# Scores over 64 features: the product with the key's lo part on 128 rows instead of 64

## The chip, the cores and the metric
The kernel runs on one core of one Trainium2 chip. The metric is the device time of one execution in microseconds; before the change three runs gave a median of 3492.87 us (3492.13 to 3494.03).

## The reference
The program computes four layers on 512 tokens of 2048 features in float32 and a last RMS norm: a layer of gated linear attention and forgetting attention, a state-space layer, a layer of a gated linear recurrence and sliding-window attention ("even"), and a layer of latent attention (MLA) and differential attention ("odd"). Every layer is a norm, a large projection, the mixers, a gate and an output projection, with the old stream added.

The change touches three score products, all of them over 64 features:
- sliding window: 16 query heads, 2 key heads of 64 features; a query block of 128 sees its own and the preceding 128 keys. `s = einsum(q, k) * 64 ** -0.5`, mask, softmax with a sink.
- MLA: 8 heads; a score is a product over 128 features of the head plus one over 64 rotary features whose key all heads share, scaled by 192 ** -0.5, causal mask, softmax.
- differential attention: 8 heads with two components of 64 features each; two causal softmaxes per head, of which one is subtracted from the other with the weight lambda. A norm over each head's 128 outputs (the "subnorm") follows.

## The kernel before
**Numbers.** A float32 operand is split into two parts of a shorter float format (float32r): hi, the rounded value, and lo, what is left. A product is then hi x hi + hi x lo + lo x hi (`PARTS`, L270), three matmuls that add in one accumulator. In projections (`chunkF` L272, `chunkT` L289) the weights are read by DMA into `wraw`, split into `whl` by ScalarE (hi) and VectorE (lo), and multiplied with the split activations `hl`; a piece's matmuls use one stationary tile twice in a row. Their accumulators are the four `pj` buffers.

**Scores over 64 features.** Two heads (or two components) lie on the two halves of the 128 partitions. `stack_q` (L210) makes one tile for each of the two: the hi part of the query in its own 64 rows, the lo part in the other 64. `stack_k` (L219) makes for each a tile with the key's hi part in both halves, and one more tile that holds the two lo parts, each in its own half. One matmul on 128 rows then gives (hi + lo) x hi; a second one on 64 rows, over the half in which the query's hi part lies, gives hi x lo. `stacked` (L228) returns these two pairs of operands:

```python
    def stacked(self, i, q, k, lo):
        h = self.HALF[i]
        return [(q, k), (q[h], lo[h])]
```

The hi copies are ScalarE's (`self.act`), the lo parts GpSimd's (`eng=self.nc.gpsimd`, called POOL in the profile).

**Where they are used.** In `layer_even`, `ev_kv` (L1279) writes both the hi and the lo part of each key head to both halves (tiles `kd` of tag hb, `kl` of tags acc and acc2). `pair` (L1302) handles two heads: for every two query tiles and each head it adds the mask by a matmul with the identity, then the two products, in one `sc` accumulator of 512 columns; softmax on VectorE and ScalarE, transposes through `tr`, value products into `po`. In `layer_odd` the rotary key is projected twice side by side (L1434 on), so `kr` (hi, tag hb) and `krl` (lo, tag acc) hold it in both halves. `mla_group` (L1459) handles two heads: projections of keys, values and queries, then for each head and each of four query tiles the plain float32 product over 128 features, the two stacked products over 1 to 4 blocks of 128 keys, and the mask (`causal_scores` L532), softmax (`softmax_tile` L510), transposes, and the value products (`pv` L541). `diff_group` (L1484) handles two heads of the differential attention: two projections with `stack_q` and `stack_k` as evacuation (tags ha for the queries and the keys' hi parts, hc for the lo parts), the value projection, then for each head and query tile two score tiles (the two components), and after the four tiles the value products and the subnorm. The subnorm squares the output, splits the square (`parts` L350, tiles of tag hc), sums it over the partitions by a matmul with ones (`rsqrt_bcast` L356) and takes the reciprocal root.

**Buffers.** The tags have fixed numbers of buffers (L109): ha 8, hb 3, hc 4, wk 4 (work tiles: evacuations and the probabilities), acc, acc2 and fac one each; accumulators pj 4, sc 2, tr 1, po 1 (L111). acc2 holds `kv_bc` and fac `q_bc` while MLA's projections run. A tile of a tag waits until an older one of that tag is no longer read.

**Order.** The program is written head by head, but the order on each engine is made by a planner (L1589), which simulates the instructions by its own costs. It puts projections of the next group between the score tiles of the group before, so TensorE works on projections while a softmax runs. Each engine takes its list in order.

Of the kernel before, what the change touches and what calls it, by code (L numbers as in the profile page):

```python
# [11 lines left out]
F32 = mybir.dt.float32  # L12
F32R = mybir.dt.float32r
# [4 lines left out]
ALU = mybir.AluOpType  # L18
# [14 lines left out]
def shape_constants():  # L33
    """Arrays that depend on shapes alone: identity, masks, rotary tables."""
# [31 lines left out]
def layout(inputs):  # L66
    """The arrays as the kernel reads them: activations by features, vectors along features as
    columns of 128, the state-space layer's by pairs of groups. Nothing is computed."""
# [31 lines left out]
class Net:  # L100
# [57 lines left out]
    @contextmanager  # L158
    def after(self, instructions):
        """Keeps what is traced inside behind these instructions on their engine."""  # L160
        with ExitStack() as st:
            for i in instructions:
                st.enter_context(self.tc.issue_after(i.ins))
            yield

# [33 lines left out]
    def split(self, dst_hi, dst_lo, src, g=None):  # L199
        """dst_hi + dst_lo = src (* g), exactly to float32."""  # L200
        if g is None:
            self.act(dst_hi, src)
            self.tt(dst_lo, src, dst_hi.bitcast(F32), ALU.subtract)
        else:
            self.act(dst_hi, src, scale=g)
            self.stt(dst_lo, src, g, dst_hi.bitcast(F32), ALU.mult, ALU.subtract)
# [3 lines left out]
    def stack_q(self, x, tags):  # L210
        """x holds two operands of 64 rows. Each gets a tile: its hi part in its own rows, its lo
        part in the others."""
        out = [self.hd(tag, F32R) for tag in tags]
        for i, h in enumerate(self.HALF):
            self.act(out[i][h], x[h])
            self.tt(out[i][self.HALF[1 - i]], x[h], out[i][h].bitcast(F32), ALU.subtract, eng=self.nc.gpsimd)
        return out

    def stack_k(self, x, tags):  # L219
        """The partners of stack_q: for each operand its hi part twice, and the lo parts in place."""  # L220
        out = [self.hd(tag, F32R) for tag in tags]
        for i, h in enumerate(self.HALF):
            for h2 in self.HALF:
                self.act(out[i][h2], x[h])
            self.tt(out[2][h], x[h], out[i][h].bitcast(F32), ALU.subtract, eng=self.nc.gpsimd)
        return out

    def stacked(self, i, q, k, lo):  # L228
        """Operands of product i: (hi + lo) * hi, then hi * lo."""
        h = self.HALF[i]  # L230
        return [(q, k), (q[h], lo[h])]

    def split_all(self, raws, gname=None, perm=False):
        """Sixteen tiles [P, S] to hi and lo parts."""
# [13 lines left out]
    CW = 256  # L248

    def wpiece(self, src, k0, n, ncol):  # L250
        """Rows of n k-tiles, split: [P, 2 parts, k-tiles, columns]."""
# [8 lines left out]
    def wcols(self, w, *segs):  # L260
        """Source of weight columns: segs are (start, width) put side by side."""
# [10 lines left out]
    def chunkF(self, h, nk, src, ncol, evac):  # L272
        """Weights stationary; evac(f, ps) gets ps [128 features, tokens]."""
# [15 lines left out]
    def chunkT(self, h, nk, src, ncol, evac):  # L289
        """Activations stationary; evac(t, ps) gets ps [128 tokens, ncol]."""  # L290
# [21 lines left out]
    def bcast(self, tok, bc=None, tag="tr"):  # L312
        """[128 tokens, 4] to [128, 512], the same row in every partition."""
# [14 lines left out]
    def colsum(self, accs, perm=False, tag="tr"):  # L328
        """Sum of accs over partitions, as [128 tokens, 4] in PSUM."""
# [8 lines left out]
    def rsqrt(self, ss, dim, mul=None):  # L338
        """rsqrt(ss / dim (* mul) + EPS) for [128, 4]."""
# [10 lines left out]
    def parts(self, x):  # L350
        hi, lo = self.hd("hc", F32R), self.hd("hc", F32R)
# [4 lines left out]
    def rsqrt_bcast(self, dim, parts, tag, bc=None):  # L356
        """rsqrt of the column sums of parts / dim + EPS, the same row in every partition."""
# [25 lines left out]
    def silu2(self, ps, bc, out=None):  # L383
        """2 * silu(ps * bc)."""
# [16 lines left out]
    def gate(self, kt0, bc):  # L401
        """Evacuation of gates: alone where they come first, else times the mixer's output."""
# [10 lines left out]
    def put(self, kt, o, col=None, row=None):  # L413
        """A mixer's output o (* col * row) to its place, times the gate if that is there."""
# [28 lines left out]
    def w_out(self, h, w, perm=False, fac=None, fold=None, store=True, beside=None):  # L443
        """x + mix @ w, feature-major. fac: factor of the old x by tokens.
        fold: gain that the new x is kept multiplied with."""
# [40 lines left out]
    def final_out(self, raws, acc, gname, out):  # L486
        """out = x * rsqrt * g."""
# [11 lines left out]
    def transpose_into(self, pt, t, probs, n, eng):  # L499
        """The n blocks of probs [128 q, n * 128], transposed, to pt's columns of tile t."""  # L500
# [9 lines left out]
    def softmax_tile(self, n, scores, scale, bias=None, rowmul=None):  # L510
        """Softmax over the n * 128 keys of one tile of queries. scores(ps) makes the
        products and the mask. Returns exp parts, 1 / sum (times rowmul)."""
# [19 lines left out]
    def causal_scores(self, t, pairs):  # L532
        """pairs: (q, k) [K, 512] operands whose products are added."""
# [7 lines left out]
    def pv(self, pt, v):  # L541
        """o [128 dv, 512]: v(kt) [128 keys, 128 dv]."""
# [9 lines left out]
    def layer_ab(self, raws, beside=None):  # L552
# [40 lines left out]
        # The first values go with the narrow columns: g_lr to rows 0-15, f_f to rows 32-39.  # L593
# [13 lines left out]
        # Decays of GLA: 16 * log_a, cumulated within chunks of 64.  # L607
# [14 lines left out]
        # log forget gates of the second attention, on partitions 32-39.  # L622
# [16 lines left out]
        # Sums of whole chunks between a token and the middle of a level's block.  # L639
# [20 lines left out]
        def gla_scores(hh):  # L660
# [3 lines left out]
            # diagonal  # L664
# [9 lines left out]
            for li, s in enumerate(LEVELS + (128, 256)):  # L674
# [9 lines left out]
                else:  # L684
# [4 lines left out]
                    for half, op in ((0, ALU.subtract), (1, ALU.add)):  # L689
                        # an access pattern keeps at most three free dimensions  # L690
# [133 lines left out]
    def s5_params(self):  # L824
        """Discretised state matrices of the state-space layer. Pairs of groups share the
        partitions as (g2, p); four steps of time make one chunk of the recurrence."""
# [21 lines left out]
        # th modulo 2 pi  # L848
# [20 lines left out]
        # exp(a) - 1 and exp(a)  # L869
# [26 lines left out]
        # (Lambda - 1) / lambda  # L896
# [16 lines left out]
        # that times Lambda ** (3 - s), s = 0 .. 2  # L913
# [18 lines left out]
        # magnitude and phase of a chunk's decay  # L932
# [5 lines left out]
        # phases of n chunks: n = 16 a + b  # L938
# [8 lines left out]
        for tab, size in ((Tb, 16), (Ta, 8)):  # L947
# [5 lines left out]
            while m < size or nxt is None:  # L953
                # pw = phase ** m; entries m .. 2m - 1
# [19 lines left out]
        # by batches: tables of phases and the magnitudes  # L974
# [13 lines left out]
    def s5_batch_params(self, b):  # L988
        """Matrices of four pairs of groups, to DRAM: C * Lambda ** (t + 1) with rows (part, p)
        and columns (g, pair, t, c); Lambda ** (3 - s) * B, real and imaginary, with rows (g, s, c)  # L990
        and columns (pair, g, p); the products within a chunk with rows (g, s, c'), columns (pair, t, c)."""
# [16 lines left out]
        # Lambda ** (3 - s) * B  # L1008
# [15 lines left out]
        # C * Lambda ** (t + 1): real part and negated imaginary part  # L1024
# [11 lines left out]
        # products within a chunk of time: rows (pair, g, c'), columns (delay, c)  # L1036
# [19 lines left out]
    def s5_batch(self, b, U, dbc, z):  # L1056
        """Four pairs of groups: U [P n, 4 pairs, (g, s, c)] to z [P channels, (t, n)]."""
# [55 lines left out]
        # states before a chunk, by groups: rows (part, p)  # L1113
# [33 lines left out]
    def layer_c(self, raws, acc):  # L1147
# [9 lines left out]
        def advance(new=None):  # L1157
            """Second half of the batch under way, once the next one's first half is there."""
# [49 lines left out]
    def layer_even(self, raws, tok, bc):  # L1208
# [7 lines left out]
        # kap = -4 * softplus(-lambda)  # L1216
# [57 lines left out]
        # sliding-window attention: two heads in a pair share the partitions  # L1274
# [27 lines left out]
        def pair(j, q):  # L1302
            kv = j // 4
            po = self.ps("po")
            for tp in range(2):
                pT2 = self.t("pt", [P, 2, S])
                pTs = [pT2[:, 0], pT2[:, 1]]
                for hf in range(2):
                    sk = sink[:, 2 * j + hf:2 * j + hf + 1]
                    pb = self.ps("sc")  # L1310
                    for a in range(2):
                        t = 2 * tp + a
                        o = a * 256
                        if t:
                            self.mm(pb[:, o:o + 256], self.identb, mb[:, 0:256], stop=False)
                            for i, (l, r) in enumerate(self.stacked(hf, q[hf], kd[kv], kl[kv])):
                                self.mm(pb[:, o:o + 256], l[:, t * P:(t + 1) * P], r[:, (t - 1) * P:(t + 1) * P], start=False, stop=(i == 1))
                        else:
                            self.mm(pb[:, 0:P], self.identb, mb[:, 256:384])
                            self.mm(pb[:, P:256], self.identb, mb[:, 128:256], stop=False)  # L1320
                            for i, (l, r) in enumerate(self.stacked(hf, q[hf], kd[kv], kl[kv])):
# [59 lines left out]
    def layer_odd(self, raws, tok, bc):  # L1381
# [3 lines left out]
        # lambda of the differential attention, in every partition  # L1385
# [29 lines left out]
        # latent projections  # L1415
# [43 lines left out]
        def mla_group(gi):  # L1459
# [13 lines left out]
            for f in range(2):  # L1473
                pt = self.t("pt", [P, 1280])
                for t in range(4):
                    pr, r = self.softmax_tile(
                        t + 1, self.causal_scores(t, [(qn[f], kn[f])] + self.stacked(f, qr[f], kr, krl)), 192 ** -0.5)
# [6 lines left out]
        def diff_group(gi):  # L1484
            qk = [None] * 4

            def ev_qk(i):
                def e(f, ps):
                    x = self.wk()
                    self.tt(x, ps, bc, ALU.mult)  # L1490
                    qk[2 * i + f] = (self.stack_k(x, ("ha", "ha", "hc")) if f else self.stack_q(x, ("ha", "ha")))
# [6 lines left out]
            for f in range(2):  # L1498
                pt = self.t("pt", [P, 1280])
                for t in range(4):  # L1500
                    wd = (t + 1) * P
                    both = []
                    for comp in range(2):
                        q, k = qk[2 * f], qk[2 * f + 1]
                        both.append(self.softmax_tile(
                            t + 1, self.causal_scores(t, self.stacked(comp, q[comp], k[comp], k[2])), 64 ** -0.5))
# [8 lines left out]
                rb = self.rsqrt_bcast(P, self.parts(sq), "tr")  # L1515
# [77 lines left out]
```

## Time and profile before

| | |
|---|---|
| median of three runs | 3492.87 us |
| the profiled execution, its span | 3490.6 us, 2.3 us less than the median of the runs |
| TensorE matmuls | 3411.1 us busy, 98%, 18156 instructions |
| weight loads (PEld, beside the matmuls) | 2829.9 us, 81% |
| VectorE, ScalarE, GpSimd | 1896.3, 1326.0, 902.8 us (54%, 38%, 26%) |
| sliding window / MLA / differential | about 1880 to 2163, 2655 to 2860, 2860 to 3265 us of the span |

PE is TensorE's matmul, PEld its weight load, DVE is VectorE, ACT ScalarE, POOL GpSimd, SP SyncE. A line such as `sc<-hc,ha 64*128 64x256 f32` is an instruction that writes a tile of the tag sc, reads hc and ha, uses 64 rows and 128 columns of the array and streams 256 columns. The profile counts a matmul as busy until its modelled end, and matmuls overlap; the distance from one start to the next is what one costs in a stream.

### The profile page before, as it was taken

What the parts mean: (1) busy time and instruction counts of PE and PEld (TensorE: products, weight loads), DVE (VectorE), ACT (ScalarE), POOL (GpSimd) and SP (SyncE); (2) the same over time, 40 slices, a digit from 0 to 9 for tenths busy, and PEclk for the clock granted to TensorE, in tenths of its full rate; (3) what the DMA queues carried; (4) which work ended last, traced back from release to release, by engine and by line L of the source; (5) the groups of instructions that cost most, each with busy time, mean ns of one, the idle gap of its engine ahead of it and who ended that gap; (6) DMA issues with size and microseconds to landing.
All of it is one profiled execution on the core that took longest, in us unless ns stands there. A gap on an engine that the chain in (4) does not pass through costs nothing.

```text
span 3490.6 us, 49294 instructions
## 1 busy us (share of the span) xinstructions
PE 3411.1 (98%) x18156; PEld 2829.9 (81%) x18156; DVE 1896.3 (54%) x3165; ACT 1326.0 (38%) x2465; POOL 902.8 (26%) x1021
## 2 busy tenths in 40 slices
PE   8999999999989999999999999999999999999997
PEld 7898788877788888888887777888888787888886
DVE  5763543475579787634354555443544545546634
ACT  4443333232332323323343554232433444445422
POOL 2341800256767665100221100012110111111011
PEclk9999999999999999999999999999999999999998
DMA  4323333467734333333442222334332222232333
GB/s 138 81 64 86 100 96 88 117 175 223 229 111 118 117 111 108 118 118 119 144 130 82 61 70 84 95 118 144 105 92 75 67 70 73 78 80 73 106 117 110
DMA packets 402849, 374.48 MB, mean 107 GB/s; under 512 B 63896, under 2 KB 364312, under 8 KB 402608
## 3 DMA queue, kind: packets, MB, share of 16 engines
q1 hardware_dynamic: 399856, 368.38, 36.4%
q8 instruction: 142, 2.33, 0.3%
q10 hardware_dynamic: 2752, 2.96, 0.3%
q14 instruction: 99, 0.81, 0.1%
HBM read 333.36 MB, written 37.86 MB: 106 GB/s over the span
## 4 chain that ended last, share of the span: by engine, by line
PE 87%; DVE 6%; POOL 3%; issue 2%; DMA 1%; ACT 1%; SPq 0%; DVEq 0%; ACTq 0%; POOLq 0%
PE pj L152 77%; PE sc L152 6%; PE po L152 3%; PE tr L156 2%; DVE wk L1107 2%; DVE wk L140 1%; DVE whl L140 1%; POOL vs L140 1%; POOL wt L140 1%; PE tr L152 1%; DVE hl L143 0%; DMA s5d<-hc 0%; SPq L265 0%; POOL hc L140 0%; DMA wraw<-in_ab_w_in_dram 0%
## 5 line engine op out<-in xcount | busy, mean ns | idle before, releaser
L152 PE MATMUL pj<-hl,whl 128*128 128x512 f32 x10224 | 2457.2, 398 | 17.5 <-ACT whl L137 8.5
L152 PEld LDWEIGHTS pj<-hl,whl 128*128 128x128 f32 x10224 | 1912.2, 189 | 463.5 <-DVE whl L140 10.9
L140 DVE TENSOR_TENSOR whl<-wraw,whl 128x512 fp32r<-128x512 f32 (+2 forms) x1064 | 838.0, 790 | 1105.2 <-ACT whl L137 1098.9
L137 ACT ACTIVATE whl<-wraw 128x512 fp32r<-128x512 f32 (+2 forms) x1064 | 661.3, 623 | 1445.7 <-PE pj L152 1192.6
L152 PE MATMUL pj<-whl,hl 128*128 128x256 f32 (+1 forms) x3840 | 488.5, 287 | 16.7 <-DVE whl L140 10.6
L152 PEld LDWEIGHTS pj<-whl,hl 128*128 128x128 f32 x3840 | 475.6, 192 | 23.1 <-DVE whl L140 11.8
L140 POOL TENSOR_TENSOR acc<-acc,wt 128x512 f32<-128x512 f32 x88 | 125.6, 1433 | 861.6 <-ACT wt L137 859.9
L140 POOL TENSOR_TENSOR ha<-wk,ha 64x512 fp32r<-64x512 f32 x32 | 44.3, 1384 | 313.9 <-ACT ha L137 272.7
L137 ACT ACTIVATE wk<-sc,sm 128x256 f32<-128x256 f32 (+3 forms) x160 | 79.5, 501 | 62.2 <-DVE sm L148 59.4
L140 POOL TENSOR_TENSOR wt<-wt,acc 64x508 f32<-64x508 f32 x32 | 57.3, 1791 | 141.7 <-DVE wt L140 85.0
L140 POOL TENSOR_TENSOR wt<-ha,wk 128x256 f32<-128x256 f32 x72 | 63.2, 905 | 112.9 <-PE pj L152 59.6
L520 DVE TENSOR_REDUCE sm<-sc 128x1 f32<-128x128 f32 (+3 forms) x96 | 47.0, 490 | 77.9 <-PE sc L152 77.5
L140 POOL TENSOR_TENSOR hc<-wt,hc 128x512 fp32r<-128x512 f32 x12 | 15.6, 1298 | 276.6 <-issue 122.3
L152 PE MATMUL po<-pt,vs 128*128 128x128 f32 x560 | 80.3, 276 | 0.0
L156 PE MATMUL tr<-ident,wk 128*128 128x128 f32 x416 | 71.3, 279 | 7.9 <-DVE wk L143 6.8
L140 POOL TENSOR_TENSOR wt<-vs,vs 128x256 f32<-128x256 f32 x64 | 58.7, 941 | 70.6 <-DMA vs<-s5w 70.0
L1107 DVE TENSOR_TENSOR_SCAN wk<-pt,wk 128x128 f32<-128x128 f32 x128 | 75.9, 656 | 0.0
L152 PEld LDWEIGHTS po<-pt,vs 128*128 128x128 f32 x560 | 72.9, 191 | 2.3
L152 PE MATMUL sc<-ha,ha 128*128 128x128 f32 (+1 forms) x224 | 72.0, 391 | 2.3 <-DVE sm L524 2.2
L156 PEld LDWEIGHTS tr<-ident,wk 128*128 128x128 f32 x416 | 52.4, 143 | 23.0 <-issue 10.1
L137 ACT ACTIVATE pt<-tr 128x256 f32<-128x256 f32 (+2 forms) x80 | 40.6, 507 | 65.9 <-PE tr L156 65.7
L148 DVE TENSOR_SCALAR wk<-wk,sm 128x256 f32<-128x256 f32 (+3 forms) x160 | 60.1, 388 | 5.0
(300 smaller groups left out, 3006.4 us busy)
## 6 DMA issues: line engine op xcount, KB each, us to landing
wraw<-in_l_w_in_dram SPq DMA_DIRECT2D x272, 256.0 KB, 2.8
wraw<-in_ab_w_in_dram SPq DMA_DIRECT2D x216, 256.0 KB, 2.8
wraw<-in_c_w_in_dram SPq DMA_DIRECT2D x128, 256.0 KB, 2.8
wraw<-in_l_w_out_dram SPq DMA_DIRECT2D x128, 256.0 KB, 2.7
wraw<-in_ab_w_out_dram SPq DMA_DIRECT2D x64, 256.0 KB, 3.8
wraw<-in_glu_w_dram SPq DMA_DIRECT2D x64, 256.0 KB, 2.6
wraw<-in_c_w_out_dram SPq DMA_DIRECT2D x64, 256.0 KB, 2.6
wraw<-in_l_w_in_dram SPq DMA_DIRECT2D x128, 128.0 KB, 2.2
```

The source lines that it names most:

```text
L137: return self.nc.scalar.activation(out, in_, func, **kw)
L140: return (eng or self.nc.vector).tensor_tensor(out, a, b, op=op)
L148: return e.tensor_scalar(out, a, s1, None, op0=op0)
L152: return self.nc.tensor.matmul(out, l, r, start=start, stop=stop)
L156: return self.nc.tensor.transpose(out, in_, self.ident[:k, :k])
L520: self.nc.vector.tensor_reduce(mx, pb[:, 0:w], axis=AX.X, op=ALU.max)
L1107: nc.vector.tensor_tensor_scan(x[:, pq(q)], tab[:, 192 + q:193 + q].to_broadcast([P, P]), x[:, pq(q)], 0.0, op0=A.mult, op1=A.add)
```

## The change
`stacked` no longer cuts the second product to 64 rows: the stacked query (hi in its half, lo in the other) is multiplied with a tile that holds the key's lo part in both halves. The result then also holds lo x lo. In the sliding-window and MLA layers such a tile is there already. In the differential attention `stack_k` makes two lo tiles per head instead of one, each with the lo part in both halves (four GpSimd operations of 64x512 instead of two, and two hc tiles instead of one). The subnorm's two parts move from hc to acc2 and fac. Comments and docstrings are taken out, which changes no instruction.

```diff
     def stack_k(self, x, tags):
         out = [self.hd(tag, F32R) for tag in tags]
         for i, h in enumerate(self.HALF):
             for h2 in self.HALF:
                 self.act(out[i][h2], x[h])
-            self.tt(out[2][h], x[h], out[i][h].bitcast(F32), ALU.subtract, eng=self.nc.gpsimd)
+            for h2 in self.HALF:
+                self.tt(out[2 + i][h2], x[h], out[i][h].bitcast(F32), ALU.subtract, eng=self.nc.gpsimd)
         return out
-    def stacked(self, i, q, k, lo):
-        h = self.HALF[i]
-        return [(q, k), (q[h], lo[h])]
+    def stacked(self, q, k, lo):
+        return [(q, k), (q, lo)]
...
-    def parts(self, x):
-        hi, lo = self.hd("hc", F32R), self.hd("hc", F32R)
+    def parts(self, x, tags=("hc", "hc")):
+        hi, lo = self.hd(tags[0], F32R), self.hd(tags[1], F32R)
...
-  for i, (l, r) in enumerate(self.stacked(hf, q[hf], kd[kv], kl[kv])):
+  for i, (l, r) in enumerate(self.stacked(q[hf], kd[kv], kl[kv])):
...
-  t + 1, self.causal_scores(t, [(qn[f], kn[f])] + self.stacked(f, qr[f], kr, krl)), 192 ** -0.5)
+  t + 1, self.causal_scores(t, [(qn[f], kn[f])] + self.stacked(qr[f], kr, krl)), 192 ** -0.5)
...
-  qk[2 * i + f] = (self.stack_k(x, ("ha", "ha", "hc")) if f else self.stack_q(x, ("ha", "ha")))
+  qk[2 * i + f] = (self.stack_k(x, ("ha", "ha", "hc", "hc")) if f else self.stack_q(x, ("ha", "ha")))
...
-  t + 1, self.causal_scores(t, self.stacked(comp, q[comp], k[comp], k[2])), 64 ** -0.5))
+  t + 1, self.causal_scores(t, self.stacked(q[comp], k[comp], k[2 + comp])), 64 ** -0.5))
...
-  rb = self.rsqrt_bcast(P, self.parts(sq), "tr")
+  rb = self.rsqrt_bcast(P, self.parts(sq, ("acc2", "fac")), "tr")
```

## Rows read from the trace of the kernel before

**Rows 1.** The page, part 1: busy us, share of span, instructions of each engine.
```profile
PE 3411.1 (98%) x18156; PEld 2829.9 (81%) x18156; DVE 1896.3 (54%) x3165; ACT 1326.0 (38%) x2465; POOL 902.8 (26%) x1021
```
**Rows 2.** Busy time by stretch: us, PE, PEld, DVE, ACT, POOL, PEclk, DMA share, GB/s.
```profile
1880.00:2163.00 283.00, 281.88 (x1385) 208.04 (x1385) 160.44 (x374) 139.94 (x325) 21.54 (x16) 1.00 0.25 70
2655.00:2860.00 205.00, 204.88 (x1091) 164.02 (x1090) 102.82 (x233) 85.68 (x184) 28.02 (x19) 1.00 0.24 64
2860.00:3265.00 405.00, 405.00 (x2218) 334.54 (x2217) 219.07 (x472) 181.62 (x361) 43.83 (x32) 1.00 0.30 80
```
**Rows 3.** Waits of TensorE, 1860 to 2170: us in total, times, longest.
```profile
PE pj L152 <- DVE wk L140: 1.1, 2, 0.6
```
**Rows 4.** Writers of the tile sc that read lo keys: min/median/max ns, starts, forms.
```profile
L152 PE MATMUL sc<-acc,ha x192: 272/275/383, 1009.0 to 2132.4; 128*128 128x128 f32 x128, 64*128 64x256 f32 x48, 64*128 64x128 f32 x16
...
L152 PE MATMUL sc<-hc,ha x64: 322/409/502, 2877.2 to 3237.0; 64*128 64x128 f32 x16, 64*128 64x256 f32 x16, 64*128 64x384 f32 x16, 64*128 64x512 f32 x16
...
L152 PE MATMUL sc<-acc,hb x32: 322/408/497, 2661.5 to 2828.9; 64*128 64x128 f32 x8, 64*128 64x256 f32 x8, 64*128 64x384 f32 x8, 64*128 64x512 f32 x8
```
**Rows 5.** Timeline of all engines at 2992.6: start us, us, engine, what, idle before.
```profile
2992.72 0.19 PEld L152 LDWEIGHTS sc<-ha,ha 128*128 128x128 f32 x1
...
2992.95 0.28 PE L152 MATMUL sc<-ha,ha 128*128 128x256 f32 x1
2993.16 0.18 PEld L152 LDWEIGHTS sc<-hc,ha 64*128 64x128 f32 x1 [0.25 <-issue]
2993.16 0.38 PE L152 MATMUL sc<-hc,ha 64*128 64x256 f32 x1
```
**Rows 6.** Timeline of TensorE's matmuls, differential attention, 2865 to 2900.
```profile
2865.79 11.44 PE L152 MATMUL pj<-whl,hl 128*128 128x256 f32 x94
2877.07 0.22 PE L152 MATMUL sc<-ha,ha 128*128 128x128 f32 x1
...
2878.05 5.59 PE L152 MATMUL pj<-hl,whl 128*128 128x512 f32 x23
2883.47 0.28 PE L152 MATMUL sc<-ha,ha 128*128 128x256 f32 x1
...
2884.68 0.94 PE L152 MATMUL pj<-hl,whl 128*128 128x512 f32 x3
...
2898.16 0.47 PE L152 MATMUL sc<-ha,ha 128*128 128x512 f32 x1
...
2899.93 0.44 PE L152 MATMUL po<-pt,vs 128*128 128x128 f32 x2
```
**Rows 7.** Chain that ended last, its longest piece: start us, us, what.
```profile
1439.19 390.41 PE pj L152 x1680
```
**Rows 8.** Timeline of TensorE's matmuls, sliding window, around 1972.
```profile
1972.14 0.28 PE L152 MATMUL sc<-maskb,identb 128*128 128x256 bf16 x1
...
1975.05 4.93 PE L152 MATMUL pj<-hl,whl 128*128 128x512 f32 x20
```
**Rows 9.** Timeline of TensorE's matmuls, MLA, 2681 to 2692.
```profile
2681.16 0.81 PE L152 MATMUL sc<-ha,ha 128*128 128x384 f32 x2
...
2682.48 3.03 PE L152 MATMUL pj<-rawb,whl 128*128 128x512 f32 x12
...
2690.64 1.05 PE L152 MATMUL po<-pt,vs 128*128 128x128 f32 x8
2691.53 0.27 PE L156 MATMUL tr<-ident,wk 128*128 128x128 f32 x1
```
**Rows 10.** The same view, forgetting attention of the first layer, around 402.
```profile
402.31 0.81 PE L152 MATMUL sc<-ha,ha 128*128 128x384 f32 x2
...
402.98 11.16 PE L152 MATMUL pj<-hl,whl 128*128 128x512 f32 x47
```
**Rows 11.** Timelines of POOL and TensorE before the last differential group's scores.
```profile
3166.62 6.05 POOL L140 TENSOR_TENSOR hc<-wk,ha 64x512 fp32r<-64x512 f32 x4
...
3180.77 0.22 PE L152 MATMUL sc<-ha,ha 128*128 128x128 f32 x1
```

More of the change, by code (lines that the diff above doesn't have):

```diff
@@ L1320, in pair @@
                             self.mm(pb[:, P:256], self.identb, mb[:, 128:256], stop=False)
-                            for i, (l, r) in enumerate(self.stacked(hf, q[hf], kd[kv], kl[kv])):
+                            for i, (l, r) in enumerate(self.stacked(q[hf], kd[kv], kl[kv])):
                                 self.mm(pb[:, P:256], l[:, 0:P], r[:, 0:P], start=False, stop=(i == 1))
```

## The prediction
> **What bounds the kernel now.** I read the page first for busy shares: TensorE's matmuls cover 98% of the span, the next engine 54% [rows 1]. That is an average, so I then asked for the three stretches in which the changed products run. In the sliding-window attention, the latent (MLA) attention and the differential attention TensorE is busy for 281.88 of 283, 204.88 of 205 and 405.00 of 405 us at a granted clock of 1.00, while VectorE is at 50 to 57% and ScalarE at 42 to 49% [rows 2]. Since matmul ends are modelled, I checked this with the waits: over the sliding-window stretch TensorE waited 1.1 us for anything that has a semaphore [rows 3]. So in these 893 us the end is set by how fast TensorE goes through its own list, and a microsecond taken out of that list is a microsecond of the kernel, as long as the other engines keep up.
>
> The next question is what the changed products cost on that list. There are 64 (48 + 16) such products on 64 rows in the sliding-window layer, 32 in MLA and 64 in the differential attention, 160 in all [rows 4]. Each stands in a group: mask, query times key-hi on 128 rows, query times key-lo on 64 rows (the mask is first or last).
>
> One group close up shows the mechanism [rows 5]. The weights of the 128-row product load from 2992.72 and its matmul starts at 2992.95: the load ran beside the matmul before. The weights of the 64-row product load from 2993.16, and its own matmul is listed from that same 2993.16: nothing was loaded ahead, the 0.18 us of load stand open.
>
> **What a group costs and what it would cost on 128 rows throughout.** I price groups from one start to the next, since durations hold modelled tails.
> - Steady rates on 128 rows: 512 columns 390.41 / 1680 = 0.2324 us [rows 7]; 256 columns (2877.07 - 2865.79) / 94 = 0.120 [rows 6]; 128 columns of float32 (2691.53 - 2690.64) / 8 = 0.111 [rows 9]. For the 128-column mask no row is clean: below it is a quarter of 0.2324 = 0.058, above 0.111; I take 0.08, near the middle.
> - Differential, two groups of 128 columns: 2877.07 to 2878.05 = 0.98, against 4 x 0.111 + 2 x 0.08 = 0.60, so 0.19 saved a group. Of 256: 2883.47 to 2884.68 = 1.21 against 0.64, so 0.285. Of 512: 2898.16 to 2899.93 = 1.77 against 1.09, so 0.34. For 384 I take 0.31, between its neighbours [rows 6]. There are 16 of each, so the mean is 0.281, and 64 x 0.281 = 18.0 us. A tail follows: the 23 projections after the first pair take 2883.47 - 2878.05 = 5.42 instead of 23 x 0.2324 = 5.35, so 0.07 for two groups, 64 x 0.037 = 2.4. Together 20.4.
> - Sliding window: four groups with three transposes, 1972.14 to 1975.05 = 2.91 [rows 8], against 12 products and masks of 256 columns x 0.120 + 3 x 0.111 = 1.77, so 0.284 a group. 48 x 0.284 = 13.6; the 16 groups of the first query tile at the 128-column price, 16 x 0.19 = 3.0; tails at half the differential's, 64 x 0.02 = 1.3. Together 17.9. No operation is added here: the lo part already lies in both halves.
> - MLA, 384 columns: 2681.16 to 2682.48 = 1.32 [rows 9]. In the forgetting attention of the first layer, which has no 64-row product, the plain float32 product of 384 columns with its mask takes 402.98 - 402.31 = 0.67 [rows 10]; with two products of 384 columns at 0.18 that makes 1.03, so 0.29 a group. Scaled as the differential's mean is to its 384 (0.281 / 0.31) and with some of the tail that is 0.28; x 32 = 9.0. Nothing is added here either.
>
> Sum: 20.4 + 17.9 + 9.0 = 47.3 us less on TensorE's list.
>
> The bounds of the operation that the trace doesn't show in this place (hi and lo product from the same stationary tile, both on 128 rows). Worst: its weights are not loaded ahead either, 0.18 us stay open 160 times, 29 us, and the gain is 18. Best: masks and 128-column products run at the column rate of 0.058, which gives 160 x 0.022 + 80 x 0.053 = 8 more, a gain of 55. I take 47, since the projections are this very pattern (one stationary tile twice in a row, loads ahead of it) at 0.120 and 0.232.
>
> The drain, as the Trainium skill has it: "TensorEngine Tiling (Array Packing)", section Key Properties, says that changing the tiling mode, and not just the tile, drains TensorE. Here the open load at 2993.16 agrees, and the price above is its price. Against the change speaks "TensorE: Matmul & The Clock Gate", section Step-by-step: a load's time goes by its columns, the row count doesn't matter; its table under Why this matters for your kernels gives a 32-row and a 128-row matmul the same time. By that alone the change would give nothing; that is the second rival below. The trace disagrees as far as the load lies open.
>
> **What is added.** Only the differential layer pays: the lo part of each key is written to both halves, 2 operations more for each of 8 heads, 16 in all, on POOL at 6.05 / 4 = 1.51 us [rows 11], 24 us of an engine that is busy 44 of 405 us [rows 2]. I cost them at nothing. What hides them is the value projection that runs before a group's first scores. The tightest group: its four lo operations end at 3166.62 + 6.05 = 3172.67; four more end at 3178.7, and the first scores start at 3180.77 [rows 11]. The stretch between holds no 64-row product, so TensorE doesn't arrive earlier. 2.1 us are left; without this cover a group would wait for the overhang, some us in each of four groups. Behind these operations on POOL stand only the next stacked operands and the two parts of the subnorm's square. The work tile that they read is held 3 us longer; there are four, shared with the probabilities.
> The subnorm's parts move to two single buffers (acc2, fac), free since the last latent projection; the second head's parts must wait for the first head's column sum, half a group earlier. Nothing.
>
> **What is late next.** TensorE reaches a tile's transposes up to 0.6 us earlier when two score groups lie between them and their scores, while the softmax chain (maximum, exp, sum, reciprocal, scaling) is as long as before. Part of the gain comes back as waits; VectorE at 57% says a small part. I take 3 us (bounds 0, and 24, half of the gain). The planner writes the order by its own costs and the added operations may move the differential layer's order: 3 us either way.
> So 47.3 - 3 = 44 us. The profiled span is 3490.6, the median 3492.87, 2.3 us around it that stay. 3492.87 - 44 = **3449**.
>
> **Rivals.**
> 1. *Waits of the softmax chain take the place.* TensorE's list is shorter, but it stops before transposes and value products. For it: in-order engine, chains of five steps. Against: 1.1 us of waits now, other engines about half busy. Price: half of the gain, 24 us; 3469.
> 2. *Rows don't matter.* The 64-row product costs what a 128-row one costs and the open load is how the profile books it. Then the lists are equal and only hidden POOL work is added: 3493. Against: the starts are measured, and 1.21 us for work that takes 0.64 elsewhere is no booking. If instead only the new product's load stays open (the worst bound), 3475.
> 3. *Slower: the hc ring.* A group now holds all four hc tiles until its last scores; before, two. The next group's keys can't be evacuated, its projections stop, and they are the cover of the softmax tiles: 23 projections, 5.35 us, between two score pairs [rows 6]. If half of 8 such gaps lose it at three group changes, 3 x 4 x 5.35 = 64 us: 3449 + 64 = 3513. It decides from 44 / 3 = 15 us a change. Against: the keys' hi parts and queries already hold all eight ha tiles just as long, so the same wait stands in the kernel now.
>
> **Chances.** Forecast (gain 34 to 56) 0.70; rival 1 (gain 10 to 34) 0.13; open load 0.05; rows don't matter 0.05; slower 0.07. A measurement of this kernel can tell 0.2%, 7 us, from no change. Faster 0.88, same 0.05, slower 0.07. The range: from the best bound, 3438, to 3468, which takes in most of rival 1 and leaves out the open load, no change and slower, 0.17.
>
> **What would show it.** Right: the score rows all say 128*128; a pair of 256-column differential groups takes about 0.65 us instead of 1.21, of 512 about 1.1; no weight load of a score starts together with its own matmul; the three stretches shrink by about 18, 9 and 20 us with TensorE still near 100%; everything outside keeps its length. POOL shows 32 lo operations of the hc tiles that end before the group's first scores. Wrong: groups as long as before (rival 2); groups short, but waits of TensorE on VectorE or ScalarE above some 10 us (rival 1); POOL or hc named as what TensorE waits for at the head of a differential group (rival 3).

## The result, and the profile after

The changed kernel takes 3449.0 us (median of 4 runs, 3445.2 to 3450.2) against 3492.5 us before; the ratio is 0.9871, interval 0.9857 to 0.9884. The profiled execution took 3447.93 us with a span of 3446.1, 44.5 us less than the span before.

Part 1 of the page of the changed kernel [rows 1], then its three stretches, cut at about the same work as before, and TensorE's waits in all three together (in total, times, longest) [rows 2, 3]:

```profile
PE 3366.5 (98%) x18156; PEld 2819.9 (82%) x18156; DVE 1896.8 (55%) x3165; ACT 1328.4 (39%) x2465; POOL 925.7 (27%) x1037
```
```profile
1880.00:2144.00 264.00, 262.88 (x1386) 202.60 (x1385) 159.31 (x375) 139.54 (x326) 21.76 (x16) 1.00 0.27 76
2636.00:2832.00 196.00, 195.88 (x1089) 163.03 (x1088) 103.13 (x233) 85.59 (x184) 32.70 (x22) 1.00 0.25 67
2832.00:3221.00 389.00, 389.00 (x2225) 332.81 (x2224) 222.25 (x473) 183.83 (x362) 64.52 (x46) 1.00 0.31 83
```
```profile
PE pj L152 <- DVE wk L140: 1.1, 2, 0.6
PE pj L152 <- DVE whl L140: 0.6, 1, 0.6
```

In the kernel before, the same view over the three stretches has the line of [rows 3] and this one:

```profile
PE pj L152 <- DVE whl L140: 0.4, 1, 0.4
```

The same 18156 matmuls take 44.6 us less of TensorE's time, and TensorE is still busy in all three stretches, each now 9 to 19 us shorter. Its waits there are 1.7 us, against 1.5 before. POOL did 16 operations and 23 us more. The three stretches by their own first and last score, from the starts of the products with key-hi (in the differential attention, of those with key-lo):

| | before | after | less |
|---|---|---|---|
| sliding window | 1889.7 to 2132.1, 242.4 us | 1889.9 to 2113.4, 223.5 | 18.9 |
| MLA | 2661.4 to 2828.2, 166.9 | 2642.6 to 2800.8, 158.2 | 8.7 |
| differential | 2877.2 to 3237.0, 359.8 | 2849.5 to 3193.4, 343.9 | 15.8 |

Behind the last score 1.4 us are gained, between the stretches 0.4; 0.2 are lost ahead of the first and 0.5 behind the last matmul.

The writers of the tile sc that read lo keys in the sliding window and the differential attention, from the changed kernel [rows 4]: no shape of 64 rows is left.

```profile
L152 PE MATMUL sc<-acc,ha x192: 270/275/382, 1009.2 to 2113.6; 128*128 128x128 f32 x144, 128*128 128x256 f32 x48
...
L152 PE MATMUL sc<-hc,ha x64: 273/320/397, 2849.5 to 3193.4; 128*128 128x128 f32 x16, 128*128 128x256 f32 x16, 128*128 128x384 f32 x16, 128*128 128x512 f32 x16
```

The same differential group as in [rows 5], timeline of all engines in the changed kernel:

```profile
2959.99 0.19 PEld L152 LDWEIGHTS sc<-ha,ha 128*128 128x128 f32 x1
...
2960.22 0.28 PE L152 MATMUL sc<-ha,ha 128*128 128x256 f32 x1
2960.22 0.19 PEld L152 LDWEIGHTS sc<-hc,ha 128*128 128x128 f32 x1
2960.34 0.28 PE L152 MATMUL sc<-hc,ha 128*128 128x256 f32 x1
2960.46 0.10 PEld L152 LDWEIGHTS <-identb 128*128 128x128 bf16 x1
2960.46 0.23 PE L152 MATMUL sc<-maskb,identb 128*128 128x128 bf16 x1
```

The lo product's weights now load from 2960.22, together with the start of the product before; its matmul starts 0.12 us later. Before, load and matmul began together, 0.21 us after the product before. The mask's weights still load together with their own matmul (2960.46), as they did in the kernel before, although the mask has 128 rows like its neighbours: an open load alone does not tell of a change of rows.

TensorE's timeline, changed kernel, differential attention [rows 6]:

```profile
2849.41 0.22 PE L152 MATMUL sc<-ha,ha 128*128 128x128 f32 x1
...
2849.92 5.59 PE L152 MATMUL pj<-hl,whl 128*128 128x512 f32 x23
2855.35 0.28 PE L152 MATMUL sc<-ha,ha 128*128 128x256 f32 x1
2855.47 0.28 PE L152 MATMUL sc<-hc,ha 128*128 128x256 f32 x1
2855.59 0.23 PE L152 MATMUL sc<-maskb,identb 128*128 128x128 bf16 x1
2855.63 0.37 PE L152 MATMUL sc<-ha,ha 128*128 128x256 f32 x1
2855.83 0.28 PE L152 MATMUL sc<-hc,ha 128*128 128x256 f32 x1
...
2856.00 0.94 PE L152 MATMUL pj<-hl,whl 128*128 128x512 f32 x3
...
2861.77 0.34 PE L152 MATMUL sc<-ha,ha 128*128 128x384 f32 x1
...
2862.68 0.44 PE L152 MATMUL po<-pt,vs 128*128 128x128 f32 x2
...
2868.89 0.47 PE L152 MATMUL sc<-ha,ha 128*128 128x512 f32 x1
2869.20 0.39 PE L152 MATMUL sc<-hc,ha 128*128 128x512 f32 x1
...
2870.09 0.44 PE L152 MATMUL po<-pt,vs 128*128 128x128 f32 x2
```

Two groups of 128, 256, 384 and 512 columns take 0.51, 0.65, 0.91 and 1.20 us; before 0.98, 1.21, 1.47 and 1.77. One detail: in the first group the lo product starts 0.12 us after its partner (2855.35 to 2855.47), in the second, right behind a mask, 0.20 (2855.63 to 2855.83).

The same cluster of the sliding window as in [rows 8] (four groups, three transposes) and of MLA as in [rows 9]:

```profile
1966.16 0.28 PE L152 MATMUL sc<-maskb,identb 128*128 128x256 bf16 x1
...
1967.94 4.80 PE L152 MATMUL pj<-hl,whl 128*128 128x512 f32 x20
1972.58 0.49 PE L156 MATMUL tr<-ident,wk 128*128 128x128 f32 x3
```
```profile
2660.79 0.81 PE L152 MATMUL sc<-ha,ha 128*128 128x384 f32 x2
...
2661.83 3.04 PE L152 MATMUL pj<-rawb,whl 128*128 128x512 f32 x12
```

1.78 us instead of 2.91, and 1.04 instead of 1.32. In the sliding window the 20 projections behind the cluster, from its end to the next transpose, took 1975.05 to 1979.81 = 4.76 us before:

```profile
1979.81 0.49 PE L156 MATMUL tr<-ident,wk 128*128 128x128 f32 x3
```

### The profile page after: what moved, and what is told of

Its sections match the earlier page's. It is cut to its first block, busy times and chain, and to the rows that moved or that the text cites. A ratio compares the mean times of both kernels' runs of the same rounds, so it can differ in the third digit from the quotient of the medians.

```text
span 3446.1 us, 49320 instructions
## 1 busy us (share of the span) xinstructions
PE 3366.5 (98%) x18156; PEld 2819.9 (82%) x18156; DVE 1896.8 (55%) x3165; ACT 1328.4 (39%) x2465; POOL 925.7 (27%) x1037
## 4 chain that ended last, share of the span: by engine, by line
PE 86%; DVE 6%; POOL 4%; DMA 2%; issue 2%; ACT 1%; SPq 0%; DVEq 0%; ACTq 0%; POOLq 0%
PE pj L152 76%; PE sc L152 4%; PE po L152 3%; PE tr L156 2%; DVE wk L1107 2%; DVE wk L140 1%; POOL pt L140 1%; POOL wt L140 1%; POOL vs L140 1%; DVE whl L140 1%; POOL hc L140 1%; PE tr L152 0%; DVE hl L143 0%; DMA s5d<-hc 0%; DMA vs<-s5w 0%
## 5 line engine op out<-in xcount | busy, mean ns | idle before, releaser
L140 POOL TENSOR_TENSOR fac<-wt,acc 128x512 fp32r<-128x512 f32 x8 | 10.4, 1294 | 236.1 <-ACT acc L137 179.2
```

The lines of the kernel that those rows point to most:

```text
L140: return (eng or self.nc.vector).tensor_tensor(out, a, b, op=op)
```

## The experiments

**One part at a time.** Three kernels made from the one before, each with one of the three score products on 128 rows, and one with the added work of the differential layer alone.

```diff
 swa_only, in pair (twice):
-for i, (l, r) in enumerate(self.stacked(hf, q[hf], kd[kv], kl[kv])):
+for i, (l, r) in enumerate([(q[hf], kd[kv]), (q[hf], kl[kv])]):
 mla_only, in mla_group:
-self.stacked(f, qr[f], kr, krl)
+[(qr[f], kr), (qr[f], krl)]
 diff_only, in diff_group, with the new stack_k (four tiles) and parts (acc2, fac):
-self.stacked(comp, q[comp], k[comp], k[2])
+[(q[comp], k[comp]), (q[comp], k[2 + comp])]
 added_only, with the same stack_k and parts, products still on 64 rows:
-self.stacked(comp, q[comp], k[comp], k[2])
+self.stacked(comp, q[comp], k[comp], k[2 + comp])
```

> Only the sliding-window scores go to 128 rows; MLA and the differential attention stay as before. If the gain is made group by group on TensorE's list, this kernel keeps what the changed kernel's trace shows for this stretch: its first score to its last takes 223.5 us instead of 242.4, so 18.9 us less, 3474 in all, and the other two stretches are as long as before. If the gain came instead from another order of the instructions in the last two layers, nothing is gained here: 3493.

> Only MLA's scores go to 128 rows. Group by group: its stretch from the first stacked score to the last shrinks from 166.9 to 158.2 us, so 8.7 us less, 3484. If order makes the gain, 3493.

> Only the differential scores go to 128 rows, with the second lo tile and the moved parts. Group by group: its stretch from first to last score shrinks from 359.8 to about 344 us, and 1.4 us lie behind it, 16 to 17.5 us in all, 3475 to 3477; the three kernels with one part each then add up to the whole change, 44 us. If the parts hide one another's waits, the sum of the three is clearly off 44.

> The differential layer's added work alone: both lo tiles in both halves, four hc tiles a group, the subnorm's parts in two single buffers, while every lo product stays on 64 rows. If the added POOL operations and buffers are hidden: 3493, within 3 us of before. If the hc ring or POOL holds a group's keys back: slower, by 10 us or more, with TensorE waiting for POOL or for hc at the head of a differential group.

Measured beside 3492.4 us for the kernel before, with the length of each stretch from its first score to its last:

| | median us | ratio, interval | sliding window | MLA | differential | behind it |
|---|---|---|---|---|---|---|
| swa_only | 3473.0 | 0.9943 (0.9928 to 0.9958) | 223.4 | 166.8 | 359.8 | 232.6 |
| mla_only | 3484.6 | 0.9977 (0.9967 to 0.9988) | 242.4 | 158.3 | 359.8 | 232.6 |
| diff_only | 3474.1 | 0.9948 (0.9932 to 0.9965) | 242.4 | 166.9 | 343.9 | 231.2 |
| added_only | 3491.8 | 1.0000 (0.9990 to 1.0009) | 242.4 | 166.9 | 361.2 | 231.4 |

Each stretch takes its new length in the kernel that changes it, and its old one to 0.1 us in the kernels that don't. The medians give 19.4, 7.8 and 18.3 us, together 45.5, against 43.5 for the whole; with the intervals of some 0.15% that is the same. The eight runs of mla_only lie between 3478.5 and 3490.7 us, wider apart than its gain, so for MLA the length of the stretch says more than the median. So the gain is made place by place, and the other order of the last layers has no part in it. The added work costs nothing that can be measured. Its trace also explains a number of the change: it lengthens the differential stretch by 1.4 us and shortens what lies behind by 1.2, so the planner only moved work over that border. Against this kernel, whose added work is the same, the change of rows alone takes 361.2 - 343.9 = 17.3 us off the stretch.

**The same products, fewer changes of shape.** The kernel before, with the sliding window's products in another order.

```diff
 in pair, for one accumulator with two query tiles (a = 0, 1), before the change:
-mask a0, hi product a0, lo product a0 (64 rows), mask a1, hi product a1, lo product a1 (64 rows)
+mask a0, mask a1, hi a0, hi a1 (128 rows), lo a0, lo a1 (64 rows)
+for i, (l, r) in enumerate(self.stacked(hf, q[hf], kd[kv], kl[kv])):
+    for n, (dst, t, ks) in enumerate(two):
+        self.mm(dst, l[:, t * P:(t + 1) * P], r[:, ks], start=False, stop=(i == 1 and n == 1))
```

> The kernel before, with the sliding window's products of one score accumulator put in another order: both masks, both products on 128 rows, then both products on 64 rows. Same products, half the changes between 128 and 64 rows (64 instead of 128). If the price lies in the change of rows, the second 64-row product costs about 0.12 us instead of 0.31 and the stretch loses about half of 18.9 us, 9 us: 3484. If a 64-row product is dear wherever it stands, because its weights never load ahead, both take 0.31 us and little is gained: at most the mask behind it, 2 to 3 us, 3490.

3483.8 us against 3494.4, ratio 0.9968 (0.9955 to 0.9981); the stretch takes 233.5 us, 8.9 less than before, 47% of the 18.9. TensorE's timeline in this kernel:

```profile
1969.31 0.39 PE L152 MATMUL sc<-maskb,identb 128*128 128x256 bf16 x2
1969.46 0.48 PE L152 MATMUL sc<-hb,ha 128*128 128x256 f32 x2
1969.87 0.50 PE L152 MATMUL sc<-acc,ha 64*128 64x256 f32 x2
1970.31 0.39 PE L152 MATMUL sc<-maskb,identb 128*128 128x256 bf16 x2
```

One alone in the kernel before, in the same layer:

```profile
1973.12 0.38 PE L152 MATMUL sc<-acc,ha 64*128 64x256 f32 x1
1973.43 0.28 PE L152 MATMUL sc<-maskb,identb 128*128 128x256 bf16 x1
```

Two 64-row products in a row take 0.44 us (1969.87 to 1970.31), one alone took 0.31 (1973.12 to 1973.43), so the second costs 0.13, about what 256 columns on 128 rows cost (0.12). The theory that a 64-row product is dear wherever it stands falls here: the price is that of the change between 128 and 64 rows. The swap also puts two masks side by side, but that is not where it gains: in the changed kernel four groups with single masks take 1.78 us, with every product, mask and transpose at its steady price 1.77.

**Where the leftover lies.** The changed kernel, with the two masks of a differential pair at its end.

```diff
-for comp in range(2):            # hi, lo, mask, softmax of each component
-    both.append(self.softmax_tile(t + 1, self.causal_scores(...), 64 ** -0.5))
+for comp in range(2):
+    for i, (l, r) in enumerate(self.stacked(q[comp], k[comp], k[2 + comp])):
+        self.mm(pbs[comp][:, 0:wd], l[:, t * P:(t + 1) * P], r[:, 0:wd], start=(i == 0), stop=False)
+for comp in range(2):
+    self.mm(pbs[comp][:, wd - P:wd], self.identb, self.maskb[:, 1], start=False, stop=True)
+both = [self.softmax_tile(t + 1, None, 64 ** -0.5, pb=pbs[comp]) for comp in range(2)]
```

> The changed kernel, with the two components' scores of the differential attention in the order product, product, product, product, mask, mask instead of product, product, mask twice. In the changed kernel the product after a mask starts its successor 0.20 us later instead of 0.12 (256 columns). If that is its weight load, for which the mask's 128 columns are too short a cover, one such place a pair goes, 32 x 0.06 = 2 us: 3447, and the third product of a pair shows 0.12. If it is the change between bf16 and float32r products whatever stands in front, the same changes are halved too, but the place behind the last mask stays: this looks alike in sum, and only the starts tell where it went. If masks cost the same wherever they stand: 3449.

3449.2 us, ratio to before 0.9868 (0.9851 to 0.9884): no difference from the changed kernel that can be measured. The 2 us of the first two expectations did not come. Its timeline:

```profile
2858.25 0.28 PE L152 MATMUL sc<-ha,ha 128*128 128x256 f32 x1
2858.36 0.28 PE L152 MATMUL sc<-hc,ha 128*128 128x256 f32 x1
2858.48 0.28 PE L152 MATMUL sc<-ha,ha 128*128 128x256 f32 x1
2858.60 0.28 PE L152 MATMUL sc<-hc,ha 128*128 128x256 f32 x1
2858.72 0.28 PE L152 MATMUL sc<-maskb,identb 128*128 128x128 bf16 x2
2858.82 0.71 PE L152 MATMUL pj<-hl,whl 128*128 128x512 f32 x2
2859.37 0.27 PE L156 MATMUL tr<-ident,wk 128*128 128x128 f32 x1
```

All products now start 0.12 us apart, so the 0.20 belonged to the place behind a mask. The pair takes 0.57 us instead of 0.65. What remains is behind the last mask: the next two projections take 0.55 us (2858.82 to 2859.37) where two steady ones take 0.46. The differential stretch and what follows are together 0.5 us shorter, below what can be told, with a new wait of 0.6 us for ScalarE. Other widths gain less than the 0.08 of this pair: summed from each start to the next, all score groups of the differential attention take 24.3 us instead of 25.4. Whether the weight load or the change of number format makes the 0.08 behind a mask stays open.

**Columns as rows.** The change and its explanation point to a further place: the sliding window's value products write 64 rows of an accumulator each and so use 64 of the array's 128 columns. The planner puts them on TensorE's list in 32 short runs between 128-column work. Here all of a pair's stand together at its end, the ones that are ready last first: 8 runs.

```diff
 in pair, changed kernel:
-    (inside the loop over tp, after the transposes of its two query tiles)
-    for a in range(2): t = 2 * tp + a; ...
-            for hf in range(2): self.mm(po[64 * hf:64 * hf + 64, ...], vt[...], pTs[hf][...])
+for t in (3, 2, 1, 0):              # after both tp
+    for i, (kt, blk) in enumerate(kts):
+        for hf in (1, 0): self.mm(po[64 * hf:64 * hf + 64, ...], vt[...], allT[tp][hf][...])
```

> The changed kernel, with the sliding window's value products (which use 64 of the 128 columns of the array, one head each) of both halves of a pair put together at the pair's end: 8 runs of such products on TensorE's list instead of 32. If every change of the array's shape has its price, columns as rows, each run that is saved gives about 0.3 to 0.5 us (around one run: 0.10 more before it, 0.15 to 0.20 more behind it, and single products that stood alone): 24 x 0.3 to 0.5 = 7 to 12 us, 3437 to 3442, faster than both kernels. If only the change of rows has a price: 3449; and if the longer wait for the last transposes of a pair is not covered: slower than 3449.

3434.4 us (3431.9 to 3435.1), ratio to before 0.9825 (0.9810 to 0.9839): 14.6 us below the changed kernel's median, and faster than both. The stretch takes 212.0 us instead of 223.5, 11.5 less. Of the 32 runs 5, and of the 8 runs 2, lie behind the last score; from the first sliding-window score to MLA's first, which takes in all of them, it is 740.0 us instead of 752.7, 12.7 less, 0.53 for each of the 24 runs saved. A run of the changed kernel and one of this kernel:

```profile
1973.00 0.43 PE L152 MATMUL po<-pt,hb 128*64 128x128 f32 x2
1973.36 0.96 PE L152 MATMUL pj<-hl,whl 128*128 128x512 f32 x3
```
```profile
1975.94 1.75 PE L152 MATMUL po<-pt,hb 128*64 128x128 f32 x28
1977.62 0.55 PE L156 MATMUL tr<-ident,wk 128*128 128x128 f32 x3
```

In a run of two a product takes (1973.36 - 1973.00) / 2 = 0.18 us, in a run of 28 it takes 1.68 / 28 = 0.06. In the long run the two heads' products, which write different halves of the accumulator's rows, start 0.007 us apart in the trace; in this run of two, 0.16. Of the 12.7 us, 6.9 lie in the value products themselves (20.3 us in the changed kernel, 13.4 here, from each start to the next) and the rest in the work beside them. The longer wait for a pair's last transposes is covered: TensorE waited 0.6 us in the three stretches. The spans of the two profiled executions differ by 12.8 us (3446.1 and 3433.3), which the 12.7 account for; the 1.8 us more between the medians lie within the scatter of the changed kernel's runs (3445.2 to 3450.2).

## Why the prediction was right

The forecast was 3449, the measured median 3449.0. That it hits to the microsecond is luck in part: two terms were off by 3 us and cancel.

- *What bounds the kernel.* Right. TensorE's list is the kernel's length in the three stretches: 44.6 us off its busy time, 44.5 off the span.
- *The price of a group*, taken as the distance from its first start to the next work less the steady price of its parts. Right in size: 0.65 us forecast and measured for the pair of 256 columns, 1.77 and 1.78 for the sliding window's cluster, 1.03 and 1.04 for MLA's. The lo product's load that stood open is gone, and the swap of the order shows that the price was the change of rows. As worded, one sign was not met: the masks' loads, which belong to the score groups, still start together with their own matmul, at no price that shows in the sliding window (1.78 against 1.77). The rule of the Trainium skill that a change of tiling mode drains TensorE ("TensorEngine Tiling (Array Packing)", Key Properties) agrees with that experiment, though no run tells a drain from a load that can't go ahead. The rule of the Trainium skill that the row count doesn't matter for a weight load ("TensorE: Matmul & The Clock Gate", Step-by-step) agrees with the loads of [rows 5], 0.18 us for 64 rows and 0.19 for 128. Nor do the rows matter for the product itself, 0.13 against 0.12; what cost the time is the change between the two.
- *Sliding window*: 17.9 forecast, 18.9 measured. The tails were taken at half of the differential's. Here the mask comes first, nothing of the group lies in front of the projections any more, and the whole tail went: 20 projections behind the cluster take 1972.58 - 1967.94 = 4.64 us, which is 20 x 0.232, instead of 4.76 before. At 0.03 for each of 64 groups that is 1.9 us where the forecast had 1.3.
- *MLA*: 9.0 forecast, 8.7 measured.
- *Differential*: the mis-sized term. 20.4 forecast, 17.3 measured for the rows alone. First, the tail of 2.4 us did not go: the 23 projections behind the first pair take 2855.35 - 2849.92 = 5.43 us after as 5.42 before, because the mask is last in the group and stands in front of them in both kernels. Second, two pairs were priced too low after the change: for 512 columns 1.20 measured against 1.09, for 384 0.91 against 0.88, since a product behind a mask starts its partner late, and so does the one behind value products (2868.89 to 2869.20); that is 0.055 x 16 + 0.015 x 16 = 1.1 less, and with the 384's price before, 1.47, the saving there is 0.28 and not 0.31, another 0.2. The pair of 128 columns was priced too high, 0.60 against 0.51, 0.045 x 16 = 0.7 more. Together 20.4 - 2.4 - 1.3 + 0.7 = 17.4. That all groups cost what the pairs do was itself a guess, since a third of them stand alone; summed from each start to the next over the stretch, the score groups take 25.4 us instead of 42.6, 17.2 less, so the gain lies in them.
- *Waits that come back, 3 us.* Wrong: waits in the three stretches went from 1.5 to 1.7 us, and all of them are waits of projections (pj), none of a transpose or a value product for the softmax chain.
- *The added work at nothing.* Right, by added_only. In the changed kernel the last group's lo operations end at 3132.07 (below), 8 us before its first score at 3140.12, where the forecast left 2.1. That is so because POOL's order changed: the lo operations of the last group's keys now stand ahead of the subnorm's part, which starts 10 us after the first of the value products that it needs (3122.20):

```profile
3125.68 6.39 POOL L140 TENSOR_TENSOR hc<-wk,ha 64x512 fp32r<-64x512 f32 x4
3132.15 1.29 POOL L140 TENSOR_TENSOR fac<-wt,acc 128x512 fp32r<-128x512 f32 x1
```

 Projections cover that too.
- *The rivals.* Waits instead of gain: 1.7 us of waits. Rows that don't matter: refuted by each of the three single parts. The hc ring: refuted by added_only, in which TensorE's only wait over the three stretches is 1.1 us of projections for VectorE.

## What to carry to other kernels

When TensorE sets the time, price its list by the distance between starts, and look for a weight load that begins together with its own matmul: here it stood at every change of the array's shape, in rows or in columns. It is a place to look and not yet a price: the masks, which differ from their neighbours in number format and not in shape, show it too, and in the sliding window it cost nothing there. A product that would leave half of the array idle is best given the full shape where its operands allow it, and otherwise put in long runs with others of its shape. Count what stands in front of the next full stream, since that part of the price stays.

## What the runs showed of the hardware

A change from 128 to 64 rows and back cost 0.27 to 0.30 us a group (17.3 / 64 and 18.9 / 64, in the layers without float32 products), more than two products of 256 columns. From 1880 to 3270 us of the kernel before, the load began within 0.007 us of its own matmul at all 383 changes of shape; in the changed kernel the same is seen at 149 masks where the shape does not change. Value products that use 64 columns of the array cost 0.18 us each in a run of two and 0.06 in a run of 28, where the products of the two heads start 0.007 us apart: a pair of them then takes 0.12, about as much as one float32 product on all 128 columns (0.11). The gain of a mere regrouping of these, 12.7 us, was a little more than expected from the starts around one run (7 to 12).
